# Layer norm and GELU on one core: the wait for the last stores behind the block's closing barrier, GpSimd not drained

## The chip, the cores and the metric

The kernel runs on one core of one Trainium2 chip. The time is device time in microseconds (us), one number per execution. The profile's span runs from the first to the last instruction of the program, so it is a little shorter than the time: before the change 318.6 us of 320.54 in the profiled execution.

## The reference

The input is 8 × 1024 rows of 2048 float32 numbers. Each row is normalised, scaled and shifted, and goes through the tanh form of GELU:

```python
mean = np.mean(x, axis=-1, keepdims=True)
var = np.var(x, axis=-1, keepdims=True)
normalized = (x - mean) / np.sqrt(var + eps)
out = gamma * normalized + beta
return (0.5 * out * (1 + np.tanh(np.sqrt(2 / np.pi) * (out + 0.044715 * out ** 3)))).astype(np.float32)
```

## The kernel before

The kernel writes one program for each of the five engines inside one block, and the block stands in a critical section of the tile framework. Sixteen batches of 512 rows go through five buffers. SyncE issues the loads, ScalarE the stores; each buffer has a semaphore that counts its stores. The last batch is stored in four pieces, one as soon as each is ready (`by_row`). At the end of its program SyncE waits until the last store of every buffer has landed. Only then does it go on to the barrier that closes the block, where all five engines meet.

```python
def stored(b):
    return sum(16 * (R if by_row(c) else 1) for c in range(b) if slot(c) == slot(b))

with tc.tile_critical(), nc.Block() as block:

    @block.sync
    def _(sy):
        for b in range(B):
            ...                                   # wait for the buffer's store, issue the load
        for b in range(B, B + SLOTS):
            sy.wait_ge(s_store[slot(b)], stored(b))

    @block.scalar
    def _(ac):
        ...
            if by_row(b):
                ins.then_inc(s_r, 1)
                ac.dma_start(out=og[b, :, q:q + 1], in_=xt[:, q:q + 1])._wait_ge(
                    s_r, b + q + 1).then_inc(s_store[slot(b)], 16)
    ...                                           # gpsimd, vector, tensor
```

Of the kernel before, what the change touches and what calls it, by code (L numbers as in the profile page):

```python
# [10 lines left out]
R = 4  # L11
# [6 lines left out]
def kernel(  # L18
# [88 lines left out]
    with tc.tile_critical(), nc.Block() as block:  # L107

        @block.sync
        def _(sy):  # L110
            for b in range(B):
                s = slot(b)
                if stored(b):
                    sy.wait_ge(s_store[s], stored(b))
                for q in range(R):
                    if b == 0:
                        sy.dma_start(out=xts[s][:, q:q + 1], in_=xg[0, :, q:q + 1]).then_inc(s_first[q], 16)
                    elif b == SPLIT:
                        sy.dma_start(out=xts[s][:, q:q + 1], in_=xg[b, :, q:q + 1]).then_inc(s_load[s], 16)
                if b not in (0, SPLIT):  # L120
                    sy.dma_start(out=xts[s], in_=xg[b]).then_inc(s_load[s], 16 * R)

            for b in range(B, B + SLOTS):
                sy.wait_ge(s_store[slot(b)], stored(b))

        @block.gpsimd
        def _(po):
            po.memset(ones, 1.0)  # L128
            po.memset(ones_b, 1.0)
            po.memset(mhalf, -0.5)  # L130
            po.memset(ident, 0.0).then_inc(s_setp, 1)
            po.affine_select(out=ident, in_=ident, compare_op=ALU.not_equal, fill=1.0, base=0,  # L132
                             pattern=[[-1, P]], channel_multiplier=1)._wait_ge(s_setp, 1).then_inc(s_setp, 1)
            with po.Fori(0, B):
                for k in range(R):
                    c = slice(k, k + 1)
                    po.tensor_scalar(out=ves[:, c], in0=mvs[:, k, 1:2], scalar1=float(eps), scalar2=1.0,  # L137
                                     op0=ALU.add, op1=ALU.mult)._wait_ge(s_a, k + 1).then_inc(s_q, 1)
                    po.tensor_tensor(out=rss[:, c], in0=ves[:, c], in1=mhalf,  # L139
                                     op=ALU.pow)._wait_ge(s_q, 2 * k + 1).then_inc(s_q, 1)  # L140
                    po.tensor_scalar(out=nms[:, c], in0=mvs[:, k, 0:1], scalar1=rss[:, c], scalar2=-1.0,  # L141
                                     op0=ALU.mult, op1=ALU.mult)._wait_ge(s_q, 2 * k + 2).then_inc(s_p, 1)
                po.sem_inc(s_a, -R)
                po.sem_inc(s_q, -2 * R)

        @block.vector
        def _(ve):
            def stats(s, q, wait, count):
                xr = xts[s][:, q].rearrange("p (s f) -> p s f", f=FMAX)
                for j in range(nsub):  # L150
                    ins = ve.bn_stats(out=sts[:, q, j, :], in_=xr[:, j, :])  # L151
                    if j == 0 and wait:
                        ins._wait_ge(*wait)
                        if wait[0] is s_load[s]:
                            ins.then_inc(s_load[s], -16 * R)
                ins.then_inc(s_o, 1)
                ve.bn_aggr(out=mvs[:, q], in_=sts[:, q])._wait_ge(s_o, count).then_inc(s_a, 1)  # L157

            def scale(q, count):
                ve.tensor_tensor(out=zgs[q % 2], in0=yks[q % 2], in1=g_t,  # L160
                                 op=ALU.mult)._wait_ge(s_n, count).then_inc(s_z, 1)
# [23 lines left out]
        def _(ac):  # L185
# [8 lines left out]
            for t in range(T + 1):  # L194
# [5 lines left out]
                if i < 0:  # L200
                    continue
# [79 lines left out]
```

## Time and profile before

| | before |
|---|---|
| time, median of 3 | 320.58 us (320.54 to 320.70) |
| span of the profiled execution | 318.6 us |
| last store issued by ScalarE | 308.945 us |
| last increment of the last store | 316.855 us |
| end of the span | 318.578 us |
| the tail: from that increment to the end of the span | 1.723 us |

Times with three decimals are single records of the trace, counted from the span's start; the printed views round to a tenth or a hundredth. The landing of a transfer is seen by its semaphore, which the sixteen DMA engines count up one by one. The prediction below shows the page, the windows of the tail, SyncE's waits and the instructions of the barrier. One line belongs beside them, the two instructions of the wait itself (line, engine, operation, count, min/median/max ns, first and last start in us; the "q" marks a sequencer instruction):

```profile
L124 SPq EVENT_SEMAPHORE  x2: 28/28/28, 307.1 to 316.9; - x2
```

There are five waits in the source and only two instructions here. Here one semaphore instruction takes two waits, and the fifth rides on the branch that leads to the barrier. The second instruction starts at 316.872 us, 17 ns after the last landing, and everything that SyncE does in the tail follows it.

### The profile page before, as it was taken

To read this page: it belongs to the slowest core of one execution; us is meant where nothing else is said; L and a number is where in the kernel's file an instruction comes from. 1 tells how busy PE (TensorE), PEld (TensorE's weight loads), DVE (VectorE), ACT (ScalarE), POOL (GpSimd) and SP (SyncE) were. 2 spreads that over 40 slices of the span, in tenths; PEclk is the share of its full clock that TensorE was granted. 3 is DMA by queue.
4 is the path that set the end of the run, shared out by engine and by line. 5 is a ranking of instruction groups with operands and counts; after the bars stand their busy time and mean duration, and the time that the engine had idled before them with its cause. 6 is when DMAs were issued, how large, how long until landed. Compare 5 with 4: busy or idle time off the path is not lost.

```text
span 318.6 us, 2087 instructions
## 1 busy us (share of the span) xinstructions
PE 244.4 (77%) x520; PEld 57.2 (18%) x520; DVE 247.5 (78%) x386; ACT 251.7 (79%) x132; POOL 110.5 (35%) x201
## 2 busy tenths in 40 slices
PE   2769999999999989686895868959688795867840
PEld 1212122222222212111221211212121121111100
DVE  4499999999999997896869968698786978859610
ACT  2769999999999989697796958959598696976860
POOL 1144444444444444233333333243232442324300
DMA  7999999999999999999999999999999999999994
GB/s 289 438 457 403 381 452 424 448 411 448 428 432 444 412 453 407 453 436 424 448 407 453 420 436 444 416 453 407 453 432 428 444 411 453 411 444 440 420 410 186
DMA packets 6002, 134.26 MB, mean 421 GB/s; under 512 B 704, under 2 KB 752, under 8 KB 752
## 3 DMA queue, kind: packets, MB, share of 16 engines
q1 hardware_dynamic: 3168, 67.11, 49.4%
q10 hardware_dynamic: 2832, 67.13, 48.9%
q14 instruction: 2, 0.02, 0.0%
HBM read 67.13 MB, written 67.11 MB: 421 GB/s over the span
## 4 chain that ended last, share of the span: by engine, by line
DMA 63%; ACT 14%; DVE 10%; POOL 5%; PE 3%; issue 1%; ACTq 0%; DVEq 0%; POOLq 0%; SPq 0%
DMA out_dram<-xt 31%; DMA xt<-in_x_dram 30%; ACT yk L197 9%; DVE sts L151 7%; ACT xt L204 4%; POOL ves L137 3%; DVE zg L160 2%; PE ps L222 2%; POOL rss L139 2%; DMA rows<-in_gamma_dram 2%; DVE mvs L157 1%; POOL nms L141 1%; PE ps L239 1%; ACT g_t L193 1%; ACTq L207 0%
## 5 line engine op out<-in xcount | busy, mean ns | idle before, releaser
L151 DVE BATCH_NORM_STATS2 sts<-xt 128x6 f32<-128x512 f32 x256 | 157.7, 679 | 32.1 <-DMA xt<-in_x_dram 30.7
L197 ACT ACTIVATE yk<-xt,nms,rss 128x2048 bf16<-128x2048 f32 x64 | 133.7, 2090 | 47.8 <-POOL nms L141 42.3
L239 PE MATMUL ps<-zg,ident 128*128 128x512 bf16 x256 | 120.8, 627 | 54.6 <-DVE zg L160 53.5
L235 PE MATMUL ps<-b_hl,ones_b 33*128 33x512 bf16 x256 | 120.6, 624 | 2.2 <-PEq L230 2.2
L204 ACT ACTIVATE xt<-ps 128x2048 f32<-128x2048 f32 x64 | 118.9, 1857 | 1.5 <-PE ps L239 1.5
L137 POOL TENSOR_SCALAR ves<-mvs 128x1 f32<-128x1 f32 x64 | 37.4, 585 | 177.9 <-DVE mvs L157 177.9
L160 DVE TENSOR_TENSOR zg<-yk,g_t 128x2048 bf16<-128x2048 bf16 x64 | 76.5, 1195 | 19.0 <-ACT yk L197 19.0
L239 PEld LDWEIGHTS ps<-zg,ident 128*128 128x128 bf16 x256 | 27.7, 130 | 147.7 <-DVE zg L160 112.4
L235 PEld LDWEIGHTS ps<-b_hl,ones_b 33*128 33x128 bf16 x256 | 27.0, 127 | 92.1 <-issue 88.4
L139 POOL TENSOR_TENSOR rss<-ves,mhalf 128x1 f32<-128x1 f32 x64 | 37.1, 580 | 5.3
L141 POOL TENSOR_SCALAR nms<-mvs,rss 128x1 f32<-128x1 f32 x64 | 34.9, 546 | 6.3
L157 DVE BATCH_NORM_AGGREGATE mvs<-sts 128x2 f32<-128x24 f32 x64 | 16.9, 264 | 2.2
L222 PE MATMUL ps<-rows,ones 1*128 1x512 f32 x8 | 7.2, 1076 | 5.9 <-DMA rows<-in_gamma_dram 5.9
L190 ACT ACTIVATE b_hl<-rows 1x2048 bf16<-1x2048 f32 x1 | 1.9, 1909 | 5.3 <-DMA rows<-in_beta_dram 5.3
L168 DVE TENSOR_TENSOR b_hl<-rows,b_hl 1x2048 bf16<-1x2048 f32 x1 | 2.3, 2281 | 3.0 <-ACT b_hl L191 3.0
L222 PEld LDWEIGHTS ps<-rows,ones 1*128 1x128 f32 x8 | 2.5, 326 | 9.0 <-DMA rows<-in_gamma_dram 5.9
L193 ACT ACTIVATE g_t<-ps 128x2048 bf16<-128x2048 f32 x1 | 1.9, 1877 | 1.8 <-PE ps L222 1.8
L186 ACT ACT_TABLE_LOAD x1 | 1.3, 1283 | 0.9 <-SPq L107 0.9
L191 ACT ACTIVATE b_hl<-rows 1x2048 bf16<-1x2048 f32 x1 | 1.9, 1908 | 0.0
L163 DVE MEMSET b_hl<- 33x1024 uint32 x1 | 0.9, 912 | 1.2 <-SPq L107 1.2
L128 POOL MEMSET ones<- 65x128 f32 x1 | 0.2, 201 | 0.5 <-SPq L107 0.5
L132 POOL TENSOR_SCALAR_AFFINE_SELECT ident<-ident 128x128 bf16<-128x128 bf16 x1 | 0.3, 292 | 0.1
(7 smaller groups left out, 0.9 us busy)
## 6 DMA issues: line engine op xcount, KB each, us to landing
out_dram<-xt ACTq DMA_DIRECT2D x15, 4096.0 KB, 33.9
xt<-in_x_dram SPq DMA_DIRECT2D x14, 4096.0 KB
xt<-in_x_dram SPq DMA_DIRECT2D x8, 1024.0 KB, 8.2
out_dram<-xt ACTq DMA_DIRECT2D x4, 1024.0 KB, 9.2
rows<-in_beta_dram ACTq DMA_DIRECT2D x2, 8.0 KB, 5.9
rows<-in_gamma_dram ACTq DMA_DIRECT2D x1, 8.0 KB, 4.9
```

The source lines that it names most:

```text
L137: po.tensor_scalar(out=ves[:, c], in0=mvs[:, k, 1:2], scalar1=float(eps), scalar2=1.0, op0=ALU.add, op1=ALU.mult)._wait_ge(s_a, k + 1).the ...
L139: po.tensor_tensor(out=rss[:, c], in0=ves[:, c], in1=mhalf, op=ALU.pow)._wait_ge(s_q, 2 * k + 1).then_inc(s_q, 1)
L141: po.tensor_scalar(out=nms[:, c], in0=mvs[:, k, 0:1], scalar1=rss[:, c], scalar2=-1.0, op0=ALU.mult, op1=ALU.mult)._wait_ge(s_q, 2 * k + 2 ...
L151: ins = ve.bn_stats(out=sts[:, q, j, :], in_=xr[:, j, :])
L157: ve.bn_aggr(out=mvs[:, q], in_=sts[:, q])._wait_ge(s_o, count).then_inc(s_a, 1)
L160: ve.tensor_tensor(out=zgs[q % 2], in0=yks[q % 2], in1=g_t, op=ALU.mult)._wait_ge(s_n, count).then_inc(s_z, 1)
L193: ac.activation(out=g_t, in_=pss[0], func=ACT.Identity)._wait_ge(s_tg, 1).then_inc(s_c, 1)
L197: ac.activation(out=yks[t % 2], in_=xts[slot(b)][:, q], func=ACT.Identity, scale=rss[:, q:q + 1], bias=nms[:, q:q + 1])._wait_ge(s_p, t + ...
L204: ins = ac.activation(out=xt[:, q], in_=pss[i % 2], func=ACT.Gelu_apprx_tanh)._wait_ge(s_t, i + 1)
L222: ins = pe.matmul(pss[0][:, cols(j)], lhsT=ones[64:65], rhs=rows[64:65, j * K // nsub:(j + 1) * K // nsub, :d // K], start=True, stop=True)
L235: ins = pe.matmul(ps[:, cols(j)], lhsT=ones_b, rhs=b_hl[:, cols(j)], start=True, stop=False)
L239: ins = pe.matmul(ps[:, cols(j)], lhsT=ident, rhs=zgs[k % 2][:, cols(j)], start=False, stop=True)
```

## The change

The intent: four engines stand at the block's barrier long before the last stores land. If SyncE joins them first and waits for the stores afterwards, the barrier runs while the stores are still moving. The flag `no_gpsimd_drain` asks the block and the critical section not to drain GpSimd. Apart from the indentation, the engine programs stay as they are.

```diff
-    with tc.tile_critical(), nc.Block() as block:
+    with tc.tile_critical(no_gpsimd_drain=True):
+        with nc.Block(no_gpsimd_drain=True) as block:
 ... (engine programs, indented by one level more)
-            for b in range(B, B + SLOTS):
-                sy.wait_ge(s_store[slot(b)], stored(b))
 ...
+        for b in range(B, B + SLOTS):
+            nc.sync.wait_ge(s_store[slot(b)], stored(b))
```

More of the change, by code (lines that the diff above doesn't have):

```diff
@@ L105, in stored @@
         return sum(16 * (R if by_row(c) else 1) for c in range(b) if slot(c) == slot(b))
-    with tc.tile_critical(), nc.Block() as block:
-        @block.sync
-        def _(sy):
-            for b in range(B):
-                s = slot(b)
-                if stored(b):
-                    sy.wait_ge(s_store[s], stored(b))
-                for q in range(R):
-                    if b == 0:
-                        sy.dma_start(out=xts[s][:, q:q + 1], in_=xg[0, :, q:q + 1]).then_inc(s_first[q], 16)
-                    elif b == SPLIT:
-                        sy.dma_start(out=xts[s][:, q:q + 1], in_=xg[b, :, q:q + 1]).then_inc(s_load[s], 16)
-                if b not in (0, SPLIT):
-                    sy.dma_start(out=xts[s], in_=xg[b]).then_inc(s_load[s], 16 * R)
-            for b in range(B, B + SLOTS):
-                sy.wait_ge(s_store[slot(b)], stored(b))
-        @block.gpsimd
-        def _(po):
-            po.memset(ones, 1.0)
-            po.memset(ones_b, 1.0)
-            po.memset(mhalf, -0.5)
-            po.memset(ident, 0.0).then_inc(s_setp, 1)
-            po.affine_select(out=ident, in_=ident, compare_op=ALU.not_equal, fill=1.0, base=0,
-                             pattern=[[-1, P]], channel_multiplier=1)._wait_ge(s_setp, 1).then_inc(s_setp, 1)
-            with po.Fori(0, B):
-                for k in range(R):
-                    c = slice(k, k + 1)
-                    po.tensor_scalar(out=ves[:, c], in0=mvs[:, k, 1:2], scalar1=float(eps), scalar2=1.0,
-                                     op0=ALU.add, op1=ALU.mult)._wait_ge(s_a, k + 1).then_inc(s_q, 1)
-                    po.tensor_tensor(out=rss[:, c], in0=ves[:, c], in1=mhalf,
-                                     op=ALU.pow)._wait_ge(s_q, 2 * k + 1).then_inc(s_q, 1)
-                    po.tensor_scalar(out=nms[:, c], in0=mvs[:, k, 0:1], scalar1=rss[:, c], scalar2=-1.0,
-                                     op0=ALU.mult, op1=ALU.mult)._wait_ge(s_q, 2 * k + 2).then_inc(s_p, 1)
-                po.sem_inc(s_a, -R)
-                po.sem_inc(s_q, -2 * R)
-        @block.vector
-        def _(ve):
-            def stats(s, q, wait, count):
-                xr = xts[s][:, q].rearrange("p (s f) -> p s f", f=FMAX)
-                for j in range(nsub):
-                    ins = ve.bn_stats(out=sts[:, q, j, :], in_=xr[:, j, :])
-                    if j == 0 and wait:
-                        ins._wait_ge(*wait)
-                        if wait[0] is s_load[s]:
-                            ins.then_inc(s_load[s], -16 * R)
-                ins.then_inc(s_o, 1)
-                ve.bn_aggr(out=mvs[:, q], in_=sts[:, q])._wait_ge(s_o, count).then_inc(s_a, 1)
-            def scale(q, count):
-                ve.tensor_tensor(out=zgs[q % 2], in0=yks[q % 2], in1=g_t,
-                                 op=ALU.mult)._wait_ge(s_n, count).then_inc(s_z, 1)
-            ve.memset(b_hl, 0.0).then_inc(s_m, 1)
-            for q in range(R):
-                stats(slot(0), q, (s_first[q], 16), q + 1)
-                if q == 0:
-                    ve.tensor_tensor(out=split(b_hl[32:33]), in0=row(32), in1=split(b_hl[32:33]),
-                                     op=ALU.subtract)._wait_ge(s_c, 2).then_inc(s_m, 1)
-                    ve.wait_ge(s_c, 3)
-                else:
-                    scale(q - 1, q)
-            ve.sem_inc(s_o, -R)
-            ve.sem_inc(s_n, -(R - 1))
-            with ve.Fori(0, (B - 1) // SLOTS):
-                for k in range(SLOTS * R):
-                    s, q = divmod(k, R)
-                    stats(s, q, (s_load[s], 16 * R) if q == 0 else None, k + 1)
-                    scale((q - 1) % R, k + 1)
-                ve.sem_inc(s_o, -SLOTS * R)
-                ve.sem_inc(s_n, -SLOTS * R)
-            scale(R - 1, 1)
-        @block.scalar
-        def _(ac):
-            ac.preload_act_table(ACT.Gelu_apprx_tanh)
-            for k, (p, src) in enumerate(((64, gamma), (0, beta), (32, beta))):
-                ac.dma_start(out=row(p), in_=src.rearrange("(o k f) -> o k f", o=1, k=K)).then_inc(s_par[k], 16)
-            ac.wait_ge(s_m, 1)
-            ac.activation(out=split(b_hl[0:1]), in_=row(0), func=ACT.Identity)._wait_ge(s_par[1], 16).then_inc(s_c, 1)
-            ac.activation(out=split(b_hl[32:33]), in_=row(32),
-                          func=ACT.Identity)._wait_ge(s_par[2], 16).then_inc(s_c, 1)
-            ac.activation(out=g_t, in_=pss[0], func=ACT.Identity)._wait_ge(s_tg, 1).then_inc(s_c, 1)
-            for t in range(T + 1):
-                if t < T:
-                    b, q = divmod(t, R)
-                    ac.activation(out=yks[t % 2], in_=xts[slot(b)][:, q], func=ACT.Identity, scale=rss[:, q:q + 1],
-                                  bias=nms[:, q:q + 1])._wait_ge(s_p, t + 1).then_inc(s_n, 1)
-                i = t - 1
-                if i < 0:
-                    continue
-                b, q = divmod(i, R)
-                xt = xts[slot(b)]
-                ins = ac.activation(out=xt[:, q], in_=pss[i % 2], func=ACT.Gelu_apprx_tanh)._wait_ge(s_t, i + 1)
-                if by_row(b):
-                    ins.then_inc(s_r, 1)
-                    ac.dma_start(out=og[b, :, q:q + 1], in_=xt[:, q:q + 1])._wait_ge(
-                        s_r, b + q + 1).then_inc(s_store[slot(b)], 16)
-                    ac.sem_inc(s_g, 1)
-                elif q == R - 1:
-                    ins.then_inc(s_r, 1)
-                    ac.dma_start(out=og[b], in_=xt)._wait_ge(s_r, b + 1).then_inc(s_store[slot(b)], 16)
-                    ac.sem_inc(s_g, 1)
-                else:
-                    ins.then_inc(s_g, 1)
-        @block.tensor
-        def _(pe):
-            pe.wait_ge(s_setp, 2)
-            for j in range(nsub):
-                ins = pe.matmul(pss[0][:, cols(j)], lhsT=ones[64:65],
-                                rhs=rows[64:65, j * K // nsub:(j + 1) * K // nsub, :d // K], start=True, stop=True)
-                if j == 0:
-                    ins._wait_ge(s_par[0], 16)
-            ins.then_inc(s_tg, 1)
-            pe.wait_ge(s_c, 3)
-            pe.wait_ge(s_m, 2)
-            pe.sem_inc(s_g, 2)
-            with pe.Fori(0, B):
-                for k in range(R):
-                    ps = pss[k % 2]
-                    for j in range(nsub):
-                        ins = pe.matmul(ps[:, cols(j)], lhsT=ones_b, rhs=b_hl[:, cols(j)], start=True, stop=False)
-                        if j == 0:
-                            ins._wait_ge(s_g, k + 1)
-                    for j in range(nsub):
-                        ins = pe.matmul(ps[:, cols(j)], lhsT=ident, rhs=zgs[k % 2][:, cols(j)],
-                                        start=False, stop=True)
-                        if j == 0:
-                            ins._wait_ge(s_z, k + 1)
-                    ins.then_inc(s_t, 1)
-                pe.sem_inc(s_g, -R)
-                pe.sem_inc(s_z, -R)
@@ new lines, with _, stats, scale @@
+    with tc.tile_critical(no_gpsimd_drain=True):
+        with nc.Block(no_gpsimd_drain=True) as block:
+            @block.sync
+            def _(sy):
+                for b in range(B):
+                    s = slot(b)
+                    if stored(b):
+                        sy.wait_ge(s_store[s], stored(b))
+                    for q in range(R):
+                        if b == 0:
+                            sy.dma_start(out=xts[s][:, q:q + 1], in_=xg[0, :, q:q + 1]).then_inc(s_first[q], 16)
+                        elif b == SPLIT:
+                            sy.dma_start(out=xts[s][:, q:q + 1], in_=xg[b, :, q:q + 1]).then_inc(s_load[s], 16)
+                    if b not in (0, SPLIT):
+                        sy.dma_start(out=xts[s], in_=xg[b]).then_inc(s_load[s], 16 * R)
+            @block.gpsimd
+            def _(po):
+                po.memset(ones, 1.0)
+                po.memset(ones_b, 1.0)
+                po.memset(mhalf, -0.5)
+                po.memset(ident, 0.0).then_inc(s_setp, 1)
+                po.affine_select(out=ident, in_=ident, compare_op=ALU.not_equal, fill=1.0, base=0,
+                                 pattern=[[-1, P]], channel_multiplier=1)._wait_ge(s_setp, 1).then_inc(s_setp, 1)
+                with po.Fori(0, B):
+                    for k in range(R):
+                        c = slice(k, k + 1)
+                        po.tensor_scalar(out=ves[:, c], in0=mvs[:, k, 1:2], scalar1=float(eps), scalar2=1.0,
+                                         op0=ALU.add, op1=ALU.mult)._wait_ge(s_a, k + 1).then_inc(s_q, 1)
+                        po.tensor_tensor(out=rss[:, c], in0=ves[:, c], in1=mhalf,
+                                         op=ALU.pow)._wait_ge(s_q, 2 * k + 1).then_inc(s_q, 1)
+                        po.tensor_scalar(out=nms[:, c], in0=mvs[:, k, 0:1], scalar1=rss[:, c], scalar2=-1.0,
+                                         op0=ALU.mult, op1=ALU.mult)._wait_ge(s_q, 2 * k + 2).then_inc(s_p, 1)
+                    po.sem_inc(s_a, -R)
+                    po.sem_inc(s_q, -2 * R)
+            @block.vector
+            def _(ve):
+                def stats(s, q, wait, count):
+                    xr = xts[s][:, q].rearrange("p (s f) -> p s f", f=FMAX)
+                    for j in range(nsub):
+                        ins = ve.bn_stats(out=sts[:, q, j, :], in_=xr[:, j, :])
+                        if j == 0 and wait:
+                            ins._wait_ge(*wait)
+                            if wait[0] is s_load[s]:
+                                ins.then_inc(s_load[s], -16 * R)
+                    ins.then_inc(s_o, 1)
+                    ve.bn_aggr(out=mvs[:, q], in_=sts[:, q])._wait_ge(s_o, count).then_inc(s_a, 1)
+                def scale(q, count):
+                    ve.tensor_tensor(out=zgs[q % 2], in0=yks[q % 2], in1=g_t,
+                                     op=ALU.mult)._wait_ge(s_n, count).then_inc(s_z, 1)
+                ve.memset(b_hl, 0.0).then_inc(s_m, 1)
+                for q in range(R):
+                    stats(slot(0), q, (s_first[q], 16), q + 1)
+                    if q == 0:
+                        ve.tensor_tensor(out=split(b_hl[32:33]), in0=row(32), in1=split(b_hl[32:33]),
+                                         op=ALU.subtract)._wait_ge(s_c, 2).then_inc(s_m, 1)
+                        ve.wait_ge(s_c, 3)
+                    else:
+                        scale(q - 1, q)
+                ve.sem_inc(s_o, -R)
+                ve.sem_inc(s_n, -(R - 1))
+                with ve.Fori(0, (B - 1) // SLOTS):
+                    for k in range(SLOTS * R):
+                        s, q = divmod(k, R)
+                        stats(s, q, (s_load[s], 16 * R) if q == 0 else None, k + 1)
+                        scale((q - 1) % R, k + 1)
+                    ve.sem_inc(s_o, -SLOTS * R)
+                    ve.sem_inc(s_n, -SLOTS * R)
+                scale(R - 1, 1)
+            @block.scalar
+            def _(ac):
+                ac.preload_act_table(ACT.Gelu_apprx_tanh)
+                for k, (p, src) in enumerate(((64, gamma), (0, beta), (32, beta))):
+                    ac.dma_start(out=row(p), in_=src.rearrange("(o k f) -> o k f", o=1, k=K)).then_inc(s_par[k], 16)
+                ac.wait_ge(s_m, 1)
+                ac.activation(out=split(b_hl[0:1]), in_=row(0), func=ACT.Identity)._wait_ge(s_par[1], 16).then_inc(s_c, 1)
+                ac.activation(out=split(b_hl[32:33]), in_=row(32),
+                              func=ACT.Identity)._wait_ge(s_par[2], 16).then_inc(s_c, 1)
+                ac.activation(out=g_t, in_=pss[0], func=ACT.Identity)._wait_ge(s_tg, 1).then_inc(s_c, 1)
+                for t in range(T + 1):
+                    if t < T:
+                        b, q = divmod(t, R)
+                        ac.activation(out=yks[t % 2], in_=xts[slot(b)][:, q], func=ACT.Identity, scale=rss[:, q:q + 1],
+                                      bias=nms[:, q:q + 1])._wait_ge(s_p, t + 1).then_inc(s_n, 1)
+                    i = t - 1
+                    if i < 0:
+                        continue
+                    b, q = divmod(i, R)
+                    xt = xts[slot(b)]
+                    ins = ac.activation(out=xt[:, q], in_=pss[i % 2], func=ACT.Gelu_apprx_tanh)._wait_ge(s_t, i + 1)
+                    if by_row(b):
+                        ins.then_inc(s_r, 1)
+                        ac.dma_start(out=og[b, :, q:q + 1], in_=xt[:, q:q + 1])._wait_ge(
+                            s_r, b + q + 1).then_inc(s_store[slot(b)], 16)
+                        ac.sem_inc(s_g, 1)
+                    elif q == R - 1:
+                        ins.then_inc(s_r, 1)
+                        ac.dma_start(out=og[b], in_=xt)._wait_ge(s_r, b + 1).then_inc(s_store[slot(b)], 16)
+                        ac.sem_inc(s_g, 1)
+                    else:
+                        ins.then_inc(s_g, 1)
+            @block.tensor
+            def _(pe):
+                pe.wait_ge(s_setp, 2)
+                for j in range(nsub):
+                    ins = pe.matmul(pss[0][:, cols(j)], lhsT=ones[64:65],
+                                    rhs=rows[64:65, j * K // nsub:(j + 1) * K // nsub, :d // K], start=True, stop=True)
+                    if j == 0:
+                        ins._wait_ge(s_par[0], 16)
+                ins.then_inc(s_tg, 1)
+                pe.wait_ge(s_c, 3)
+                pe.wait_ge(s_m, 2)
+                pe.sem_inc(s_g, 2)
+                with pe.Fori(0, B):
+                    for k in range(R):
+                        ps = pss[k % 2]
+                        for j in range(nsub):
+                            ins = pe.matmul(ps[:, cols(j)], lhsT=ones_b, rhs=b_hl[:, cols(j)], start=True, stop=False)
+                            if j == 0:
+                                ins._wait_ge(s_g, k + 1)
+                        for j in range(nsub):
+                            ins = pe.matmul(ps[:, cols(j)], lhsT=ident, rhs=zgs[k % 2][:, cols(j)],
+                                            start=False, stop=True)
+                            if j == 0:
+                                ins._wait_ge(s_z, k + 1)
+                        ins.then_inc(s_t, 1)
+                    pe.sem_inc(s_g, -R)
+                    pe.sem_inc(s_z, -R)
+        for b in range(B, B + SLOTS):
+            nc.sync.wait_ge(s_store[slot(b)], stored(b))
```

## The prediction

> **What bounds the kernel now.** I read the page first: engine shares, the DMA line of the slices, the chain.
>
> ```profile
> span 318.6 us, 2087 instructions
> ...
> PE 244.4 (77%) x520; PEld 57.2 (18%) x520; DVE 247.5 (78%) x386; ACT 251.7 (79%) x132; POOL 110.5 (35%) x201
> ...
> DMA  7999999999999999999999999999999999999994
> GB/s 289 438 457 403 381 452 424 448 411 448 428 432 444 412 453 407 453 436 424 448 407 453 420 436 444 416 453 407 453 432 428 444 411 453 411 444 440 420 410 186
> ...
> HBM read 67.13 MB, written 67.11 MB: 421 GB/s over the span
> ```
>
> No engine is busy over 79% of the span, while the sixteen DMA engines are full in every slice but the first and the last. The kernel is bound by moving 134 MB. The change touches no transfer, buffer or compute instruction, so 3 to 314 us should stay as they are; the question is the last slice, where DMA falls to four tenths. I then cut the tail into windows (columns: stretch, length, busy time and count of PE, PEld, DVE, ACT, POOL, then clock, DMA share, GB/s).
>
> ```profile
> 309.00:314.00 5.00, 0.00 (x0) 0.00 (x0) 0.00 (x0) 0.00 (x0) 0.00 (x0) 1.00 1.00 421
> 314.00:316.50 2.50, 0.00 (x0) 0.00 (x0) 0.00 (x0) 0.00 (x0) 0.00 (x0) 1.00 0.06 26
> 316.50:318.60 2.10, 0.00 (x0) 0.00 (x0) 0.00 (x0) 0.00 (x0) 0.00 (x0) 1.00 0.00 0
> ```
>
> From 309 us on nothing computes: for 5 us the last stores move at full rate, then comes a short remainder, and in the last 2.1 us nothing computes and nothing is moved. That last stretch is pure bookkeeping, and only it can become shorter. The waits of SyncE's queue, from 300 us on (who, for what, total us, times, longest), say what it begins with:
>
> ```profile
> SPq L124 <- DMA out_dram<-xt: 64.6, 2, 54.9
> SPq L276 <- PEq L276: 0.7, 2, 0.6
> SPq L107 <- PEq L107: 0.2, 1, 0.2
> ```
>
> Line 124 is the wait for the last stores, ahead of the barrier that closes the block of engine programs (booked on line 107, where the block is opened). So the order now is: stores land, SyncE goes on, and only then the barrier of line 107 is completed. The instructions of line 107 (operation, count, min/median/max ns, first and last start) show what that barrier consists of:
>
> ```profile
> L107 SPq EVENT_SEMAPHORE  x4: 17/22/28, 317.2 to 317.5; - x4
> ...
> L107 POOLq DRAIN  x2: 41/330/619, 300.3 to 317.4; - x2
> L107 DVEq DRAIN  x2: 19/642/1266, 303.8 to 317.4; - x2
> L107 PEldq DRAIN  x2: 13/705/1397, 305.7 to 317.4; - x2
> L107 ACTq DRAIN  x2: 8/40/73, 309.4 to 317.4; - x2
> L107 SPq DRAIN  x2: 7/7/7, 317.1 to 317.4; - x2
> L107 POOLq EVENT_SEMAPHORE  x2: 17/17/17, 317.1 to 317.2; - x2
> L107 SPq COMPARE_BRANCH  x1: 33/33/33, 316.9 to 316.9; - x1
> ```
>
> Each engine has two DRAINs here: the first at the block's barrier, the second at the exit of the critical section, all at 317.4 us. The first ones are long past on GpSimd (300.3), VectorE (303.8), TensorE (305.7) and ScalarE (309.4); only SyncE's is at 317.1, behind the stores. Four engines stand at the barrier for 8 to 17 us and wait for SyncE. This is what the change wants to use.
>
> **What the skill says.** The page "DMA: Bandwidth & Descriptors", section "Why a DMA increments its semaphore by 16 and not by 1", says that only the full sixteen increments mean that all data has landed. The trace agrees: of the last store's increments the fifteenth comes at 314.807 us, the sixteenth 2.05 us later at 316.855, and SyncE's wait at line 124 ends at 316.872, 17 ns after it. So the wait itself cannot move earlier, wherever it stands in the program. "Perfetto Trace Analysis", section "Sequencer-only Instruction (DRAIN, etc)", says that only the execution of such an instruction is reported, neither its wait nor the propagation of its semaphore. The trace agrees: SyncE's DRAIN is given as 7 ns, but its next instructions follow by 65 to 73 ns. I therefore never add durations; I count from start to start. "VectorE: DVE Perf Modes", section "The DRAIN you can't avoid", gives the DRAINs of the frame as a constant of about 12 ns. In this trace that holds for engines that are already idle (7 to 19 ns), except GpSimd, at 34 to 97 ns at the end; a DRAIN behind unfinished work lasts longer (619 ns on GpSimd at 300.3 us, 1397 on TensorE at 305.7).
>
> **Part 1: the wait behind the barrier.** The individual records of the trace give this path from the landing to the signal that starts the critical section's exit (starts, in us): 316.872 SyncE's wait for two of the store semaphores; 316.945 a branch, on which its last such wait rides; 317.098 its DRAIN; 317.130 GpSimd sees that all have arrived; 317.209 GpSimd releases; 317.250 SyncE sees the release; 317.315 SyncE gives the exit signal. The steps are 73, 153, 32, 79, 41 and 65 ns, together 443 ns. After it, the exit's DRAINs, three gathering instructions of SyncE, then the two barriers of the program's end with the clearing of the semaphores between them (all booked on line 276) last from 317.315 to 318.578, that is 1.263 us; the change leaves them where they are.
>
> After the change SyncE arrives at the block's barrier when its last load has been issued (251.9 plus 0.35 us). The last to arrive is then ScalarE, whose DRAIN starts at 309.404 and lasts 73 ns; with the same 32 + 79 + 41 ns all are released by some 309.65. This lies 7 us before the landing, beside the last stores. After the landing only the wait and the exit signal are left. I have two counts for it. If the third wait rides on an ordinary semaphore instruction or on the signal itself, the signal follows the wait by 65 to 73 ns: saved 443 minus 65 to 73, so 370 to 378 ns. If it rides on a branch again, as in the kernel before, 73 + 153 = 226 ns remain and 443 minus 226 = 217 ns are saved. No view tells how the program will be laid out; I take the two as about equally likely: (374 + 217) / 2 = 296, rounded to 0.3 us.
>
> **Part 2: GpSimd is not drained.** At the block's barrier its DRAIN of 619 ns starts at 300.282 and ends at 300.901, still 8 us before ScalarE arrives: worth nothing. At the exit, its DRAIN (317.357, 41 ns) lies beside the other four: SyncE's own is at 317.398 and TensorE's at 317.413, and SyncE collects GpSimd's mark last, at 317.602, when it has been there since 317.407. Worth nothing in time; at most one collecting instruction of SyncE less, 67 to 74 ns by the spacing here (317.535, 317.602, 317.676). It would need GpSimd's mark to go too, and I give that little weight: some 10 ns in the mean. GpSimd's DRAINs on line 276 (34, 97, 34 ns) belong to the program's end and stay, as I read the diff.
>
> **Sum.** 320.58 minus 0.3 is 320.28 us: 0.1% faster. The re-indentation of the engine programs changes no instruction in them.
>
> **The rivals.** First, **nothing at all is gained**: a barrier that moved under the stores is replaced by another that costs the same, since the exit still needs the landing, an engine-wide exchange and two barriers at the end. For it speaks that 1.26 of the 1.72 us after the landing stay. Against it speaks that the exit exchange and the end's barriers are in the trace already, after the removed one (DRAINs of line 107 at 317.4 and those of line 276 at 317.5 and later). It would make 320.5 to 320.7. Second, **a much larger gain**, were GpSimd's drain the expensive part and on the path: 0.6 us more, so 319.6. The trace speaks against it: the 619 ns DRAIN is at 300.3 us, and the one that comes late takes 41. Third, **the stores themselves end at another time**: an earlier start of SyncE's polling, another code layout or other instruction fetches could shift when loads and stores mix; a shift of the last landing goes one to one into the time. For this speaks that the sum of many transfers decides the end; against it, that the issue instructions are unchanged and three runs of before lie within 0.16 us. I give it plus or minus 0.25 us. Fourth, **a slower exit**, if the four parked engines had to fetch their instructions anew or a wait took two instructions more: some 0.07 us for each, too little to turn the sign.
>
> **Range and chances.** The mechanism gives 0.2 to 0.45 us, so 320.13 to 320.38; with the scatter of the runs and the third rival I take 320.0 to 320.6 for eight times in ten. Two per cent are 6.4 us, over three times all the time after the last landing (1.72 us), and no buffer or order of transfers changes. So a change within 2% is nearly certain: 0.99, with 0.005 on either side.
>
> **What will show it.** Right: the DRAINs of line 107 on SyncE start once near 252 us and once after the landing; the barrier's release on all engines is at about 309.6; from the sixteenth increment of the last store to the end of the span it takes 1.3 to 1.5 us in place of 1.72; GpSimd has fewer DRAINs on that line. The groups of compute instructions and the moved bytes are the same, the last landing within 0.3 us of 316.9. Wrong would be: a stretch from landing to end still over 1.65 us (first rival), or under 1.2 us (the exit or the end's barriers changed too), or a last landing that moved by more than the tail was shortened.

## The result

The changed kernel took 320.17 us (median of 4, 319.99 to 321.05), the kernel before 320.64 (median of 4, 320.54 to 321.05). The ratio is 0.9988, with a 95% interval from 0.9968 to 1.0009. Ratios here are the mean time of one kernel's fast runs over that of the other's fast runs of the same rounds, so they are not quite the ratios of the medians. By the time alone the change is not clear of the noise. The trace is much sharper. These are the lines of the page that answer to those of before:

```profile
span 318.5 us, 2090 instructions
...
PE 244.3 (77%) x520; PEld 57.2 (18%) x520; DVE 247.5 (78%) x386; ACT 251.7 (79%) x132; POOL 110.6 (35%) x201
...
DMA  7999999999999999999999999999999999999995
...
HBM read 67.13 MB, written 67.11 MB: 421 GB/s over the span
```

Counts of compute instructions and moved bytes are the same, and the DMA engines are as full. The windows of the tail, by the same cuts as before (length, busy time and count of PE, PEld, DVE, ACT, POOL, then clock, DMA share, GB/s):

```profile
309.00:314.00 5.00, 0.00 (x0) 0.00 (x0) 0.00 (x0) 1.29 (x1) 0.00 (x0) 1.00 1.01 421
314.00:316.50 2.50, 0.00 (x0) 0.00 (x0) 0.00 (x0) 0.00 (x0) 0.00 (x0) 1.00 0.21 88
316.50:318.60 2.10, 0.00 (x0) 0.00 (x0) 0.00 (x0) 0.00 (x0) 0.00 (x0) 1.00 0.00 0
```

In this execution the last GELU reaches past 309 us, 1.4 us later than in the profiled one of before. The last data packet ends at 316.58 us (316.41 before), which the rounded share of the last window does not show. SyncE's waits (who, for what, total us, times, longest) show the new order:

```profile
SPq L108 <- PEq L108: 59.6, 1, 59.6
SPq L247 <- DMA out_dram<-xt: 5.9, 1, 5.9
```

SyncE now first waits 59.6 us at the barrier of line 108, and only then, for the last 5.9 us, for the stores (line 247, behind the block). The instructions of the block's barrier, which now has the line of the block (108), and of the exit from the critical section (107):

```profile
L108 SPq EVENT_SEMAPHORE  x2: 17/17/17, 251.5 to 311.1; - x2
...
L108 POOLq EVENT_SEMAPHORE  x2: 17/17/17, 310.9 to 311.0; - x2
L108 SPq DRAIN  x1: 223/223/223, 251.2 to 251.2; - x1
...
L108 ACTq DRAIN  x1: 83/83/83, 310.8 to 310.8; - x1
```

```profile
L107 SPq COMPARE_BRANCH  x1: 33/33/33, 317.1 to 317.1; - x1
...
L107 POOLq NOP  x1: 17/17/17, 317.3 to 317.3; - x1
```

SyncE arrives at the barrier at 251 us, and the barrier is over at 311.1 us, six microseconds before the last landing. GpSimd has no DRAIN at the exit any more but a NOP. The wait's last part rides on a branch again. The path after the landing, from the records of the two traces:

| start, us | before | after |
|---|---|---|
| last increment of the last store | 316.855 | 317.034 |
| wait ends | 316.872 | 317.051 |
| branch with the last wait | 316.945 | 317.118 |
| SyncE's DRAIN at the barrier | 317.098 | (at 251.2) |
| GpSimd has all arrivals | 317.130 | (at 310.942) |
| GpSimd releases | 317.209 | (at 311.021) |
| SyncE is released | 317.250 | (at 311.062) |
| SyncE's exit signal | 317.315 | 317.273 |
| end of the span | 318.578 | 318.535 |
| **tail** | **1.723** | **1.501** |

From the wait's end to the signal it is 443 ns before and 222 ns after. From the signal to the end it is 1.263 us and 1.262 us. The tail is shorter by 0.222 us, exactly the barrier's part. In this pair of traces most of it is covered up by a last landing that came 0.179 us later.

The time can thus be written as a sum of three terms: the last landing, the tail, and what is outside the span. Each execution lists its span (to a tenth), so the third term is known for every run. It showed something that I had not looked for: 1.945 us in the mean of 25 runs of the kernel before, but 1.820 in the 4 runs of the changed one. The experiments had to explain this too.

### The profile page after: what moved, and what is told of

Read it like the earlier page. It is cut to its first block, busy times and chain, and to the rows that moved or that the text cites. A ratio compares the mean times of both kernels' runs of the same rounds, so it can differ in the third digit from the quotient of the medians.

```text
span 318.5 us, 2090 instructions
## 1 busy us (share of the span) xinstructions
PE 244.3 (77%) x520; PEld 57.2 (18%) x520; DVE 247.5 (78%) x386; ACT 251.7 (79%) x132; POOL 110.6 (35%) x201
## 4 chain that ended last, share of the span: by engine, by line
DMA 64%; ACT 14%; DVE 10%; POOL 5%; PE 3%; issue 1%; ACTq 0%; DVEq 0%; POOLq 0%; SPq 0%
DMA xt<-in_x_dram 32%; DMA out_dram<-xt 30%; ACT yk L195 9%; DVE sts L149 7%; ACT xt L202 4%; POOL ves L135 3%; DVE zg L158 2%; PE ps L220 2%; DMA rows<-in_gamma_dram 2%; POOL rss L137 2%; POOL nms L139 1%; DVE mvs L155 1%; PE ps L237 1%; ACT g_t L191 1%; ACTq L205 0%
## 5 line engine op out<-in xcount | busy, mean ns | idle before, releaser
L135 POOL TENSOR_SCALAR ves<-mvs 128x1 f32<-128x1 f32 x64 | 38.5, 602 | 179.2 <-DVE mvs L155 179.2
L139 POOL TENSOR_SCALAR nms<-mvs,rss 128x1 f32<-128x1 f32 x64 | 35.7, 558 | 6.3
L137 POOL TENSOR_TENSOR rss<-ves,mhalf 128x1 f32<-128x1 f32 x64 | 35.3, 552 | 5.3
```

Of the source, the lines that this page charges most:

```text
L135: po.tensor_scalar(out=ves[:, c], in0=mvs[:, k, 1:2], scalar1=float(eps), scalar2=1.0, op0=ALU.add, op1=ALU.mult)._wait_ge(s_a, k + 1).the ...
L137: po.tensor_tensor(out=rss[:, c], in0=ves[:, c], in1=mhalf, op=ALU.pow)._wait_ge(s_q, 2 * k + 1).then_inc(s_q, 1)
L139: po.tensor_scalar(out=nms[:, c], in0=mvs[:, k, 0:1], scalar1=rss[:, c], scalar2=-1.0, op0=ALU.mult, op1=ALU.mult)._wait_ge(s_q, 2 * k + 2 ...
```

## The experiments

My theory after the result: the barrier's 0.222 us is all that the moved wait gives, and it gives it wholly; the flags give nothing. The rivals: the flags have a share; the transfers moved; SyncE's instructions in the tail are not really what the end waits for. Twelve kernels were run, four to a call (a1 to a3 with a5, a4 with b1 to b3, c1 to c4), each call beside runs of the kernel before on the same chip. The three calls ran on three chips. All twelve gave correct results.

| run | median us | before, median us | ratio (95%) | tail, us | outside the span, mean us |
|---|---|---|---|---|---|
| before | | | | 1.723 | 1.945 |
| changed, first measured | 320.17 | 320.64 | 0.9988 (0.9968 to 1.0009) | 1.501 | 1.820 |
| a1, changed, again | 320.35 | 320.66 | 0.9991 (0.9978 to 1.0005) | 1.501 | 1.774 |
| a2, wait moved only | 320.32 | 320.66 | 0.9994 (0.9980 to 1.0007) | 1.516 | 1.936 |
| a3, flags only | 320.42 | 320.66 | 0.9989 (0.9975 to 1.0002) | 1.782 | 1.808 |
| a4, no wait on a branch | 320.10 | 320.56 | 0.9986 (0.9971 to 1.0001) | 1.426 | 1.800 |
| a5, last wait alone | 320.07 | 320.66 | 0.9979 (0.9966 to 0.9993) | 1.340 | 1.756 |
| b1, twenty behind the wait | 321.50 | 320.56 | 1.0036 (1.0020 to 1.0051) | 2.534 | 1.767 |
| b2, twenty ahead of the barrier | 320.28 | 320.56 | 0.9994 (0.9979 to 1.0009) | 1.512 | 1.768 |
| b3, wait behind everything | 318.45 | 320.56 | 0.9936 (0.9922 to 0.9949) | 0.033 | 1.348 |
| c1, block's flag only, wait moved | 320.24 | 320.48 | 0.9995 (0.9979 to 1.0012) | 1.501 | 1.827 |
| c2, section's flag only, wait moved | 320.47 | 320.48 | 1.0010 (0.9993 to 1.0026) | 1.516 | 1.962 |
| c3, no flags, four engines one longer | 320.32 | 320.48 | 0.9995 (0.9978 to 1.0011) | 1.516 | 1.813 |
| c4, both flags, GpSimd one longer | 320.38 | 320.48 | 0.9994 (0.9977 to 1.0011) | 1.501 | 1.818 |

The tail is that of each profiled execution. The last column is the mean of time less span over all runs of the kernel (4 or 5, 25 for before).

### The changed kernel again (a1)

No edit.

> The changed kernel once more, for a narrower interval of the time. My theory (the barrier of the block runs beside the last stores, 0.222 us less from the last landing to the end of the span, nothing else): tail 1.50 us again to within 0.02, mean time 0.1 to 0.35 us below before, the rest of any difference being a last landing that scatters by some 0.3 us. Rival (the change also moves the transfers, as 320.17 against 320.64 might hint): a mean time 0.4 to 0.6 us below before, with last landings that are earlier in the changed kernel.

The tail was 1.501 us again, to the nanosecond, and the mean time 0.26 us below before. The last landing was at 317.316 us, later than in the profile of before, so the rival of earlier transfers finds no support. Span less tail gives a mean landing of 316.91 us for the 25 runs of before and of 317.10 for the 9 of the changed kernel, with single runs scattering by more than 0.2 us. The other kernels with a moved wait help little: call by call, their mean landing (a1 included) is 0.01, 0.20 and 0.18 us later than that of before. Whether the landing is really a little later after the change is not settled; there is no sign that it is earlier.

### The two parts alone (a2, a3)

a2 has the moved wait without flags:

```diff
-    with tc.tile_critical(no_gpsimd_drain=True):
-        with nc.Block(no_gpsimd_drain=True) as block:
+    with tc.tile_critical():
+        with nc.Block() as block:
```

> Only the wait is moved behind the barrier; both barriers drain GpSimd as before. My theory: tail 1.50 us (within 0.03 of the changed kernel), since GpSimd's drain was never on the path; time as the changed kernel within 0.2 us. Rival (GpSimd's drain has a share in the gain): tail 1.55 to 1.72 us.

GpSimd is drained again, at the block's barrier as before:

```profile
L108 POOLq DRAIN  x1: 621/621/621, 301.5 to 301.5; - x1
```

Its 621 ns lie 15 us ahead of the landing, and the tail is 1.516 us. The moved wait brings 0.207 of the 0.222 us. The other 0.015 us is not a drain: c1 below, which drains GpSimd at the exit, has 1.501 us again, and c2, which does not, has 1.516. What makes it stays open (b2, with both flags, has 1.512).

a3 is the changed kernel with the wait put back in place:

```diff
+                for b in range(B, B + SLOTS):
+                    sy.wait_ge(s_store[slot(b)], stored(b))
 ...
-        for b in range(B, B + SLOTS):
-            nc.sync.wait_ge(s_store[slot(b)], stored(b))
```

> Only the two flags; the wait stands in SyncE's program ahead of the barrier, as before. My theory: nothing is gained, and the tail grows from 1.72 to about 1.79 us, because with the flag an engine arrives at the block's barrier with two instructions (a DRAIN, then a semaphore instruction, 65 to 73 ns later) in place of one, and SyncE's arrival is on the path here. Rival (the flags are worth something by themselves): tail below 1.70 us.

The tail grew to 1.782 us, close to the 1.79 expected. The barrier's instructions of SyncE show why:

```profile
L108 SPq EVENT_SEMAPHORE  x2: 17/17/17, 317.6 to 317.8; - x2
...
L108 SPq COMPARE_BRANCH  x1: 33/33/33, 317.4 to 317.4; - x1
L108 SPq DRAIN  x1: 7/7/7, 317.5 to 317.5; - x1
```

SyncE arrives with a DRAIN and, 58 ns later by the records, a semaphore instruction. Without the flag the DRAIN itself announces the arrival. So inside the span the flags alone make the kernel slower by 0.059 us. The measured time does not follow that: the ratio is 0.9989, with 1 still inside the interval. The last column explains part of it, since this kernel too spends less time outside the span, 1.808 us. That was the point at which my theory of the flags had a hole.

### What an instruction behind the landing costs (a5, a4, b1, b2)

a5 leaves the four older waits in SyncE's program, and the last one gets an instruction of its own:

```diff
+                for b in range(B, B + SLOTS - 1):
+                    sy.wait_ge(s_store[slot(b)], stored(b))
 ...
-        for b in range(B, B + SLOTS):
-            nc.sync.wait_ge(s_store[slot(b)], stored(b))
+        b = B + SLOTS - 1
+        nc.sync.wait_ge(s_store[slot(b)], stored(b))
+        nc.sync.sem_inc(s_tg, 1)
```

> The changed kernel, with the four waits for older stores put back into SyncE's program ahead of the barrier (they are over by 307 us), and the last wait alone behind the barrier, on a semaphore instruction of its own, so that no branch carries a wait. My theory (after the landing each instruction of SyncE counts one to one: 67 ns wait to branch, 155 ns branch to signal): the signal follows the wait by 65 ns in place of 222, so the tail is 1.34 us, 0.157 less than in the changed kernel and 0.38 less than before. Rival (the branch is only the profile's booking, or the parked engines are the limit): tail 1.45 to 1.50 us.

The tail was 1.340 us, as expected. The signal follows the wait by 57 ns in place of 222. The ratio of 0.9979 is clear of the noise, so this kernel is faster than before, by 0.66 us in the mean. Its tail accounts for 0.383 and the time outside the span for 0.19; the remaining 0.09 is an earlier mean landing, well inside the scatter of single runs.

a4 only adds an instruction behind the five waits of the changed kernel:

```diff
         for b in range(B, B + SLOTS):
             nc.sync.wait_ge(s_store[slot(b)], stored(b))
+        nc.sync.sem_inc(s_tg, 1)
```

> The changed kernel with one semaphore instruction behind the five waits. The waits then ride on three semaphore instructions and none on a branch, and the wait that ends last on the second of them. My theory: signal 65 + 67 = 132 ns after the wait in place of 222, tail 1.41 us: half way to the kernel with the last wait alone, and one instruction more than the changed kernel has makes it faster. Rival (one instruction more costs one more): tail 1.56 us.

The tail was 1.426 us. One instruction more than in the changed kernel made the tail 0.075 us shorter, since the fifth wait no longer needs a branch. That is a little less than the expected 0.09: the step from the added instruction to the signal was 76 ns, not 65.

b1 adds twenty such instructions in place of one.

```diff
         for b in range(B, B + SLOTS):
             nc.sync.wait_ge(s_store[slot(b)], stored(b))
+        for _ in range(20):
+            nc.sync.sem_inc(s_tg, 1)
```

> The changed kernel with twenty semaphore instructions of SyncE behind the wait for the last stores, ahead of the exit signal (they count up a semaphore that nobody waits for any more). My theory: one to one on the path, 59 to 67 ns each, less the branch that no longer carries a wait: tail 1.50 + 1.2 to 1.3 - 0.09 = 2.6 to 2.75 us, and the time 1.0 to 1.3 us above the changed kernel. Rival (SyncE's instructions here overlap with something else that ends last): tail and time up by less than half of that.

```profile
L249 SPq EVENT_SEMAPHORE  x20: 17/17/28, 317.1 to 318.2; - x20
```

The tail was 2.534 us, a little below the expected range. Nineteen more than in a4 cost 1.108 us, 58 ns each, and this is one to one on the path. My figure of 59 to 67 ns was a little high; the reported 17 ns of each is less than a third of what it costs. The time rose with it, to 1.0036 times before.

b2 has the twenty ahead of the barrier.

```diff
                         sy.dma_start(out=xts[s], in_=xg[b]).then_inc(s_load[s], 16 * R)
+                for _ in range(20):
+                    sy.sem_inc(s_tg, 1)
```

> The same twenty semaphore instructions, but in SyncE's program ahead of the barrier, behind its last load. My theory: SyncE has some 60 us to spare there, so the tail stays 1.50 us and the time is that of the changed kernel within 0.3 us. Rival: any more costs as much as behind the wait, 1.2 us.

The tail was 1.512 us and the time that of the changed kernel. The same work costs over 1 us behind the landing and nothing ahead of it. This settles what the change lives on.

### The idea carried to its end (b3)

The four stores of the last batch count on a semaphore from outside the tile framework, so that the clearing at the program's end does not touch it. SyncE waits for it as the very last thing and sets it back to zero.

```diff
-                            s_r, b + q + 1).then_inc(s_store[slot(b)], 16)
+                            s_r, b + q + 1).then_inc(s_fin, 16)
 ...
+    s_fin = nc.alloc_semaphore("fin")
     with _tile.TileContext(nc) as tc:
-        tile_layer_norm_gelu_kernel(tc, *args)
+        tile_layer_norm_gelu_kernel(tc, *args, s_fin)
+    nc.sync.wait_ge(s_fin, 16 * R)
+    nc.sync.sem_inc(s_fin, -16 * R)
```

(The waits for the older stores went back into SyncE's program, ahead of the barrier. The semaphore is also a new argument of the kernel function.)

> The idea carried to its end: the four stores of the last block count on a semaphore of their own, allocated outside of the tile context, and SyncE waits for it behind the two barriers and the clearing of semaphores at the program's end; the older stores are waited for in SyncE's program. My theory (everything that does not need the data can run beside the last stores): the tail shrinks from 1.50 to about 0.04 us, and the time is 1.3 to 1.5 us below the changed kernel, 1.5 to 1.8 below before, 0.5 per cent. Rival (the stores end at another time, or what follows the program takes up what the tail gave): the span shrinks, but the time by less than half of it.

The instructions of the program's end (line 282 here, 276 before) and the wait:

```profile
L282 POOLq EVENT_SEMAPHORE  x4: 17/17/17, 311.5 to 312.2; - x4
...
L282 POOLq EVENT_SEMAPHORE_RANGE_CLEAR  x1: 226/226/226, 311.8 to 311.8; - x1
```

```profile
L285 SPq EVENT_SEMAPHORE  x1: 17/17/17, 317.2 to 317.2; - x1
```

Both barriers of the end and the clearing now take place near 312 us, and one instruction of 17 ns is left after the landing: tail 0.033 us. The median is 318.45 us, and the ratio of 0.9936 is clear of the noise. This kernel beats both others, by 2.05 us in the mean against before. I had expected 1.5 to 1.8. The excess comes from outside the span: 1.348 us in place of about 1.8 in the changed kernel and 1.94 in before. (Tail and outside together would give 2.28 us; a mean landing 0.23 us later than in before's runs of this call takes the rest back.) The trace shows how. After the span a semaphore that no instruction of the program names is counted up in two rounds of nine; I take this for the runtime's own closing barrier. In b3 its first four counts already come at 312.6 to 312.8 us, when the other four engines have left the program, and the fifth at 317.331 us, after SyncE's wait. In the changed kernel all of them come after the span.

Only the results of these runs vouch for b3, all correct; no other test was made of letting the program's end begin while stores still move.

### What shortens the time outside the span (c1 to c4)

By now every kernel with the block's flag, b3 apart, had 1.76 to 1.82 us outside the span, and the two without (before and a2) 1.94 to 1.95. The flag also changes the number of instructions: PE, DVE, ACT and SP get one more each (the separate arrival at the barrier), GpSimd one less (the drain). Theory A was GpSimd's length, theory B its drains. The edits:

```diff
 c1:   tile_critical(no_gpsimd_drain=True) -> tile_critical()
 c2:   nc.Block(no_gpsimd_drain=True)      -> nc.Block()
 c3:   a2, and  sem_inc(s_tg, 1)  at the end of the sync, vector, scalar and tensor programs
 c4:   the changed kernel, and  po.sem_inc(s_tg, 1)  at the end of the gpsimd program
```

What was expected of c1:

> The runs so far leave something over: the time outside the span (a run's time less its span) is 1.94 to 1.95 us in the mean for the two kernels without flags (before, 18 runs; the wait moved alone, 5 runs) and 1.76 to 1.82 for those with flags, although the tail inside the span does not tell them apart. Here the wait stands behind the barrier and only the block has the flag. Theory A (the length of GpSimd's program, which the block's flag makes one instruction shorter, shifts something in what follows the program): 1.76 to 1.82 us outside. Theory B (the flag of the critical section does it, since that removes the DRAIN that comes after the landing): 1.93 to 1.96. Tail under both: 1.50 us.

Of c2:

> The reverse: wait behind the barrier, only the critical section has the flag (GpSimd's DRAIN at the exit becomes a NOP, no engine's count of instructions changes). Theory A (length of the program): 1.93 to 1.96 us outside the span, as without flags. Theory B (the DRAIN at the exit): 1.76 to 1.82. Tail under both: 1.50 to 1.52 us.

Of c3:

> The kernel with the wait moved alone, no flags, and one semaphore instruction more at the end of the programs of TensorE, VectorE, ScalarE and SyncE, which gives these four the number of instructions that the flags give them; GpSimd's program is that of the kernel without flags. If the four engines' lengths matter: 1.76 to 1.82 us outside the span. If GpSimd's length or its DRAINs matter: 1.93 to 1.96. Tail 1.50 to 1.52 us under both, since the added ones run beside the last stores.

Of c4:

> The changed kernel with both flags and one semaphore instruction more at the end of GpSimd's program, so that it is as long again as without flags, still without the two DRAINs. Theory A (GpSimd's length): 1.93 to 1.96 us outside the span, as without flags, and a time 0.15 us above the changed kernel's. Theory B (a DRAIN of GpSimd, wherever): 1.76 to 1.82 us. Tail 1.50 us under both.

c1 had 1.827 us and c2 1.962: the block's flag does it, the section's flag does nothing, as theory A said. But c4 had 1.818 with GpSimd's program as long as before, so theory A falls. And c3 had 1.813 without any flag and with all of GpSimd's drains, so theory B falls too. What all short ones have in common, and the three long ones (before, a2, c2) lack, is at least one instruction more on the other four engines. More than one on SyncE (b1 and b2 have twenty) brings nothing further.

The means of the table suffer from spans that are listed to a tenth. In the profiled executions the span is known to the nanosecond, and they separate the kernels cleanly. In the first call a2 has 1.930 us outside, a1, a3 and a5 have 1.783 to 1.789; in the third call c2 has 1.958, the others 1.809 to 1.818. So the effect is about 0.145 us in both. In the traces 0.123 us of it sit in one place: in the last round of the closing barrier, the last step but one takes 157 to 158 ns in the three long kernels and 34 to 35 ns in all others. Another step, between the two rounds, takes 0.785 to 0.789 us in the profiles of the changed kernel and of the first two calls, and 0.815 to 0.818 in those of the third call and of before. It goes with the call and not with the flag (a2 has 0.786, c1 0.818), so the 0.177 us between the profiles of before and after overstate the flag's share by 0.03.

"Runtime: NRT & Kernel Launch", section "The ~15µs preamble/postamble breakdown", gives about 355 ns for a round over the five engines in the barrier ahead of the kernel. The last round of the closing barrier took 356 ns in the changed kernel and 481 ns in the one before; the first round took 524 ns in both. Which of the four engines' programs has to be longer, and by what mechanism that step gets faster, these runs do not tell. As far as they go, the table's third term depends on the number of instructions in these four programs and not on GpSimd's drains.

## Why the prediction was right

The time of 320.17 us lies inside the range of 320.0 to 320.6, and "within 2%" came true. Step by step:

- **What bounds the kernel.** Right. In the changed kernel each engine's busy time agrees to 0.1 us and the moved bytes are the same, and the last landing stayed between 316.5 and 317.4 us in all fourteen profiles, while ScalarE issued the last store anywhere from 308.9 to 312.1 us. The queue of transfers sets the landing, not the issue of the last store.
- **Part 1, the moved wait.** Right in mechanism. In size the lower of its two counts held, since the wait rode on a branch again: 217 ns predicted for that case, 222 measured, 207 in a2. The average of 0.3 us was too high, and the tail of 1.501 us lies at the very edge of the 1.3 to 1.5 that it named. The other count is what a5 realises (383 ns). "Advanced Engine Details and Errata", section "Control Flow Timing", gives about 108 ns for a compare-and-branch; here the step from this branch to the next instruction was 153 ns before and 155 after. One reading of the prediction is a little off: what follows SyncE's 7 ns DRAINs directly comes 63 and 73 ns later, not 65 to 73. And the DRAINs that it holds against the page's 12 ns are those of the block and the program's end, while the page speaks of the runtime's own.
- **"All are released by some 309.65".** Off, 311.1 in the trace. ScalarE's last store was issued 1.4 us later in that execution, and with the flag the arrival takes two instructions, which I had not seen. It lies beside the stores and cost nothing.
- **Part 2, "worth nothing".** Right about the drains, wrong about the flag. GpSimd's drains were never on the path (a2, c3). But the block's flag shortened what comes after the span by some 0.15 us, by adding an instruction to the other engines. My sum contained the span only. With this term the sum is 0.222 + about 0.15 = 0.37 us; the means of the two measurements of the changed kernel lie 0.37 and 0.26 below before. That they stand so close to the predicted 0.3 is luck: the tail gave less than 0.3, and a term that I did not know made up for it.
- **The rivals.** "Nothing at all is gained" falls with the records of the tail and with a5, whose time is clear of the noise. "A much larger gain" by the drain falls with a2. "The stores end at another time" is true of single executions and was of the size that I gave it, but no kernel shows a shift that stands out of the scatter. "A slower exit" did not come: 1.263 and 1.262 us from signal to end.

A change of 0.1% cannot be shown by the times of nine runs here. It is shown by the tail, which repeats to a nanosecond, and by the variants that make the same mechanism larger (b1, b3).

## What to carry to other kernels

Look at what happens between the last landing and the end of the span, and ask of each instruction there whether it needs the data. What doesn't need it can stand ahead of the wait, beside the last transfers, at no cost; here that was worth 0.2 us for one barrier and 2.05 us for all of it. Judge a change of this size by the records of the trace and by an enlarged variant, not by the time of a few runs, and look outside the span as well.

## What the Trainium skill lacked or had wrong

- No page gives the distance, from start to start, of semaphore instructions that follow one another on SyncE. "Perfetto Trace Analysis", section "Sequencer-only Instruction (DRAIN, etc)", says that the reported duration leaves out part of it, without a number. Here one with a reported 17 ns costs 58 ns behind the last wait (nineteen cost 1.108 us).
- "Advanced Engine Details and Errata" gives about 108 ns for a compare-and-branch. Here one that carries a wait, long met, takes 151 to 155 ns to the next instruction (before, after, a2, a3). Without it the tail is 0.075 us shorter with one instruction more (a4) and 0.161 us shorter with the last wait alone (a5).
- "Runtime: NRT & Kernel Launch" gives about 355 ns for the round of the barrier ahead of the kernel and no such figure for the closing one. Here the closing barrier's last round took 356 to 358 ns in the kernels with one instruction more on four engines and 480 to 481 ns in the others (one step of 158 ns). The stages that the page lists after the kernel add up to about 5 us; the traces here show 1.90 to 2.06 us from the end of the span to the last count of that barrier (b3 apart), and whether anything follows it they do not show. No page says that this part can begin while stores are still moving, as in b3, which has 0.45 us less outside the span than the changed kernel's kind.
- "VectorE: DVE Perf Modes" gives about 12 ns, constant on all engines, for the DRAINs that the runtime puts around a kernel, and has nothing on those that the block and the program's end bring with them (lines 107 and 276 here). Of these GpSimd's took 34 to 97 ns at the program's end, and those behind unfinished work up to 1397 ns (TensorE at the block's barrier).
- "DMA: Bandwidth & Descriptors" says that a transfer's engines finish independently, but not by how much. In the trace of before the sixteenth increment of a store came 0.19 us after the fifteenth at 76 us, 1.78 at 271 us and 2.05 at the end; in that of the changed kernel it was 1.67 at the end. The wait for the last engine alone is thus longer than all the bookkeeping that this change moved (0.222 us).
